# Three edits to hand-written instruction orders in the differential-attention part of a two-layer trunk: a score block issued earlier, a group-norm matmul issued later, a copy issued later

## The chip, the cores and the metric

The kernel runs on one core of a Trainium2 chip, in one launch. The metric is the device time of that core in microseconds (us), as the median of several executions; a profile of one execution stands beside it. The engines are PE (TensorE, matrix products), DVE (VectorE), ACT (ScalarE), POOL (GpSimd) and SP (SyncE, which issues most DMA transfers).

## The reference, cut to what matters

Two layers work on one sequence of 1024 tokens with 1024 features. Layer 0 mixes the tokens by differential attention, layer 1 by latent attention (MLA); each is followed by a gated MLP with a short convolution. All edits lie in layer 0's attention, which is this:

```python
def diff_attention(h, w_qkv, ..., subln_g, w_o, lambda_init, cos, sin):
    q, k, v = jnp.split(h @ w_qkv, 3, axis=-1)      # 8 heads, each two query/key maps of 64
    ...                                             # rotary on q and k, lam from four vectors
    def block(args):                                # 128 queries
        sc = jnp.einsum('bqhcd,bkhcd->bhcqk', qb, k).astype(jnp.float32) * scale
        p = masked_softmax(sc, chunk_mask(blk, s)[None, None, None])
        a = p[:, :, 0] - lam * p[:, :, 1]
        return jnp.einsum('bhqk,bkhe->bqhe', a.astype(v.dtype), v)
    ...
    o = rms_norm(o, subln_g) * (1.0 - lambda_init)  # the group norm, over a head's 128 features
    return o.reshape(b, s, D_MODEL) @ w_o
```

The input `h` is `rms_norm(x, attn_norm_g[0])`, so each token row is multiplied by a norm vector first.

## The kernel before

Every product of float32 values is made of three matmuls on high and low parts (`mm3`, lines 119 to 121: high by low, high by high, low by high).

**Steps.** The attention has 32 steps `t = 4h + p`: head `h`, query pair `p`. A pair is two rows of 128 queries, `j = 0` and `j = 1`; row `i = 2p + j` sees the first `n = 128(i + 1)` keys. For each step the code holds small pieces of work under letters: `S0`, `S1` the scores of the two rows (L1859: for both maps, on 64 partitions each, three passes of a pair of matmuls); `M` masks and takes the maximum (DVE, L1868 and L1869); `E` the exponentials (ACT, L1884); `I` the inverse of the sums (DVE, L1889, L1890); `C` scales the first map (POOL, L149, for pairs 0 and 1); `X` subtracts the second map (DVE, L1897); `T` transposes the result (PE, L1905), `H` and `L` split it into high and low (ACT L127, DVE L130); `A` multiplies by the values (PE); `O` copies out (ACT, L1933). At the end of every second pair comes the group norm: `Q1`, `Q2`, `Q3` square and split (ACT L1939, L1942, POOL L130), `F` sums over the 128 features with a matrix of ones (PE, L1950 and L1951), and `R`, `N` take the root and scale (ACT L1957 to L1961, DVE). A prime behind a letter means the step before, two primes the step before that; a plus means the step after.

**Projections.** Between these pieces stand the two halves of up to two projection units per step, `U` and `V`, which make a half of the next queries, keys or values: `U0` and `U1` are 24 matmuls into a PSUM bank with the tag `u`, of which there is one. For queries and keys, `Us` (a shuffle, DVE L596) and `Um` (times the cosine, DVE L600) read that bank, `Up` and `Ua` (POOL, L617) finish the rotary, `Uqh` and `Uql` (ACT L127, POOL L130) split the query. `V0` opens the same bank for the second unit.

**Order.** `da_steps` runs a row of letters per step under a hand-written schedule, so each of PE, DVE, ACT and POOL executes its instructions in exactly the order of the row. Rows 0 to 3 of `DA_SCORE` serve the pairs 0 to 3; `DA_SECOND` replaces row 1 at `t = 1`; the rows of `DA_END` serve the last steps, `t = 28` on, where the output projection's pieces (small letters, and `Y`, `Z`) are mixed in. The row of pair 1 serves `t = 5, 9, 13, 17, 21, 25`; at `t = 29` a row of `DA_END` is used.

**Score buffers.** Scores go to PSUM tiles of two banks with the tag `S`, of which there are two. For pairs 0 and 1 a row's two maps share one tile; for pairs 2 and 3 each map takes one, so that `S0` alone takes both.

**The start.** `FIRST` is the order before the steps. For tile `i` of 128 tokens: `Q` squares (ACT L157), `R` the root (DVE L164, POOL L167), `N` times the norm vector (DVE L439), `T`, `H`, `L` transposes and splits of a half (`a`, `b`; PE L447, ACT L127, DVE L130). `g` spreads the norm vector over a score tile in PSUM; `G` (ACT, L509) copies it from there to SBUF, where `N2` to `N7` read it. `p10a` and `p10b` are the two halves of the first key projection, which need the `a` halves and the `b` halves of tiles 0 and 1; `z` are filling matmuls on ones (L195).

Of the kernel before, what the change touches and what calls it, by code (L numbers as in the profile page):

```python
# [56 lines left out]
class Trunk:  # L57
# [234 lines left out]
    def steps(self, attend, units, prepare, n, apart=False):  # L292
# [33 lines left out]

    DA_SCORE = (
# [4 lines left out]
    )  # L332

    DA_SECOND = "S0 I1' Vc' H2'' M0 L2'' A1'' C0' X0' H3'' E0b L3'' U0 E0a A2'' Wh Vt' N3'''' A3'' O'' Wl' Q2'' C1' I0 X1' U1 C0 S1 X0 Us Vh' Q1'' T0' H0' Q3'' Up F'' Um M1 Ua Wl R1'' Vl' E1b V0 E1a L0' I1 A0' Uqh R2'' R3'' Uql C1 N1'' X1 V1 T1 T0 H0"

    DA_END = (
# [9 lines left out]
    def da_steps(self, attend, units, prepare, n, extra):  # L346
# [4 lines left out]
        with self.tc.manual_schedule(engines={E.PE, E.DVE, E.Activation, E.Pool}):  # L351
            for t in range(-1, first + len(self.DA_END)):
                while len(steps) < min(n, t + 2):
# [3 lines left out]
                    for name, u in zip("UV", units(x)):  # L357
                        steps[x].parts.update({name + part: f for part, f in u.items()})
                row = self.DA_SECOND if t == 1 else self.DA_SCORE[t % 4] if t < first else self.DA_END[t - first]
                for name in row.split():  # L360
# [6 lines left out]
        assert not extra and not any(s.parts for s in steps)  # L367

    FIRST = (
# [1939 lines left out]
```

## Time and the profile before

| | |
|---|---|
| median of 3 runs | 2386.59 us (2385.97 to 2387.23) |
| profiled execution, its own time | 2385.1 us |
| its span, first to last instruction | 2383.2 us |
| PE busy | 2349.0 us, 99% |
| DVE, ACT, POOL busy | 1917.6, 1245.7, 586.2 us |
| mean granted TensorE clock | 0.998 |
| start (`FIRST`) | to about 42 us |
| steps of layer 0's attention | about 42 to 472 us |

An instruction's start and end are given in us from the span's start. Matmuls overlap: the time one costs PE is the step from its start to the next one's start, not the duration in its row. "Idle before" names what the engine waited for.

### The profile page before, as it was taken

Reading aid. Unit: us, or ns where it says so; the run is one execution under the profiler, and the core shown is the slowest. Engines: PE = TensorE matmul, PEld = TensorE weight load, DVE = VectorE, ACT = ScalarE, POOL = GpSimd, SP = SyncE. Lnnn points to the kernel's source line nnn. Section 1 sums busy time; section 2 is a strip of 40 time slices with the busy share of each in tenths; the row PEclk is TensorE's granted clock in tenths of the full one; section 3 lists DMA queues with packets and bytes.
Section 4 is the critical chain, followed back from the end, with each engine's and each line's share of the span. In section 5 each row is a group of like instructions: output and inputs, shape, how many; then the busy total and the mean of one; then the engine's idle time right before and its main releaser. Section 6 shows DMA issues by size and latency. Waiting matters only on the chain.

```text
span 2383.2 us, 32951 instructions
## 1 busy us (share of the span) xinstructions
PE 2349.0 (99%) x12146; PEld 1979.3 (83%) x12146; DVE 1917.6 (80%) x3169; ACT 1245.7 (52%) x2301; POOL 586.2 (25%) x466
## 2 busy tenths in 40 slices
PE   9999999999999999999999999999999999999998
PEld 8888888788888888888898889988788888887886
DVE  6777877758888888899865888886588888888997
ACT  5666666735444444354444778775354444443544
POOL 4545444324000000000133666673320000000001
PEclk9999999999999999999999999999999999999999
DMA  3111111332222222652221211133322222227502
GB/s 147 40 36 36 49 36 54 115 111 102 94 83 80 80 89 80 234 167 92 83 99 56 71 32 39 41 98 106 114 74 95 80 80 80 89 80 282 177 1 80
DMA packets 95666, 213.42 MB, mean 90 GB/s; under 512 B 8712, under 2 KB 33936, under 8 KB 95504
## 3 DMA queue, kind: packets, MB, share of 16 engines
q1 hardware_dynamic: 86304, 183.51, 23.5%
q10 hardware_dynamic: 9200, 27.80, 3.2%
q8 instruction: 96, 1.57, 0.3%
q14 instruction: 66, 0.54, 0.1%
HBM read 158.85 MB, written 52.43 MB: 89 GB/s over the span
## 4 chain that ended last, share of the span: by engine, by line
PE 89%; DVE 5%; DMA 2%; issue 1%; POOL 1%; ACT 1%; SPq 0%; DVEq 0%; POOLq 0%; ACTq 0%
PE S L119 13%; PE S L121 13%; PE S L120 13%; PE b L119 8%; PE b L120 8%; PE b L121 8%; PE u L119 5%; PE u L121 4%; PE u L120 4%; PE S L1859 3%; PE b L263 2%; PE u L2015 1%; PE u L2014 1%; PE b L1905 1%; DVE s L130 1%
## 5 line engine op out<-in xcount | busy, mean ns | idle before, releaser
L167 POOL TENSOR_TENSOR st<-st,mhalf 128x1 f32<-128x1 f32 x56 | 35.3, 632 | 1299.1 <-DVE st L164 1290.6
L119 PE MATMUL S<-s,u 128*128 128x512 f32 (+1 forms) x800 | 302.1, 378 | 1.8 <-DVE s L130 1.8
L121 PE MATMUL S<-s,u 128*128 128x512 f32 (+1 forms) x800 | 301.2, 377 | 1.5 <-DVE u L130 0.8
L120 PE MATMUL S<-s,u 128*128 128x512 f32 (+1 forms) x800 | 301.0, 376 | 0.0
L127 ACT CAST u<-h 128x512 fp32r<-128x512 f32 (+1 forms) x194 | 115.9, 619 | 273.8 <-DVE h L1012 271.9
L119 PE MATMUL b<-s,u 128*128 128x512 f32 x588 | 230.8, 393 | 1.2 <-DVE s L130 0.4
L121 PE MATMUL b<-s,u 128*128 128x512 f32 x588 | 229.1, 390 | 0.0
L120 PE MATMUL b<-s,u 128*128 128x512 f32 x588 | 229.0, 389 | 0.0
L1069 DVE SCALAR_TENSOR_TENSOR u<-u,conv,u 128x1023 f32<-128x1023 f32 (+1 forms) x176 | 224.9, 1278 | 0.8 <-ACT u L1065 0.7
L149 POOL TENSOR_TENSOR u<-u,st 128x512 f32<-128x512 f32 (+7 forms) x160 | 172.2, 1085 | 158.2 <-DVE st L2000 106.7
L127 ACT CAST s<-u 128x512 fp32r<-128x512 f32 (+3 forms) x229 | 144.3, 663 | 94.0 <-PE u L121 26.4
L127 ACT CAST u<-b 128x512 fp32r<-128x512 f32 (+1 forms) x256 | 134.7, 547 | 93.3 <-PE b L1905 58.5
L130 DVE TENSOR_TENSOR u<-b,u 128x512 fp32r<-128x512 f32 (+1 forms) x256 | 158.5, 631 | 25.1 <-ACT u L127 24.0
L119 PEld LDWEIGHTS S<-s,u 128*128 128x128 f32 x800 | 150.5, 188 | 30.1 <-DVE s L130 2.4
L121 PEld LDWEIGHTS S<-s,u 128*128 128x128 f32 x800 | 150.5, 188 | 29.2 <-DVE u L130 1.0
L120 PEld LDWEIGHTS S<-s,u 128*128 128x128 f32 x800 | 150.5, 188 | 27.4
L119 PE MATMUL u<-s,s 128*128 128x512 f32 (+1 forms) x408 | 165.1, 405 | 0.9 <-DVE s L130 0.7
L121 PE MATMUL u<-s,s 128*128 128x512 f32 (+1 forms) x408 | 158.3, 388 | 0.0
L120 PE MATMUL u<-s,s 128*128 128x512 f32 (+1 forms) x408 | 157.6, 386 | 0.0
L130 DVE TENSOR_TENSOR s<-u,s 128x512 fp32r<-128x512 f32 (+2 forms) x204 | 138.9, 713 | 11.1 <-ACT s L127 10.7
L1072 ACT ACTIVATE u<-u 128x1024 f32<-128x1024 f32 x44 | 46.7, 1062 | 187.3 <-DVE u L1069 187.3
L130 DVE TENSOR_TENSOR u<-h,u 128x512 fp32r<-128x512 f32 x171 | 117.4, 687 | 32.6 <-ACT u L127 31.5
(288 smaller groups left out, 6382.5 us busy)
## 6 DMA issues: line engine op xcount, KB each, us to landing
u<-in_ffn_up SPq DMA_DIRECT2D x88, 512.0 KB, 4.1
g_d<-u ACTq DMA_DIRECT2D x44, 512.0 KB, 2.6
u<-in_ffn_down SPq DMA_DIRECT2D x66, 256.0 KB, 4.9
u<-g_d SPq DMA_DIRECT2D x62, 256.0 KB, 4.1
s<-in_da_wqkv SPq DMA_DIRECT2D x23, 512.0 KB, 3.3
x_d<-u SPq DMA_DIRECT2D x16, 512.0 KB, 2.9
s<-x_d SPq DMA_DIRECT2D x8, 1024.0 KB, 10.6
u<-o_d SPq DMA_DIRECT2D x24, 256.0 KB, 3.1
```

The source lines that it names most:

```text
L119: mm(out, lh, rl, start=first, stop=False, skip_group_check=onto)
L120: mm(out, lh, rh, start=False, stop=False, skip_group_check=onto)
L121: mm(out, ll, rh, start=False, stop=last, skip_group_check=onto)
L127: self.nc.scalar.copy(out, src)
L130: (eng or self.nc.vector).tensor_sub(out, src, hi.bitcast(F32))
L149: self.nc.gpsimd.tensor_mul(x, x, s.to_broadcast(list(x.shape)))
L167: nc.gpsimd.tensor_tensor(r, s, self.mhalf, ALU.pow)
L263: self.nc.tensor.transpose(ps[:, j * P : (j + 1) * P], probs[t][:, k : k + P], self.ident)
L1069: nc.vector.scalar_tensor_tensor(t[half][:, back:], u[half][:, : S - back], w, t[half][:, back:], ALU.mult, ALU.add)
L1072: nc.scalar.activation(t[0], t[0], AF.Silu)
L1859: nc.tensor.matmul(sc[c][:, b : b + m], q[rows, qp, qs], kt[rows, kp, :m], start=x == 0, stop=x == 2)
L1905: k.nc.tensor.transpose(ps[:, j * P : (j + 1) * P], self.e[t][0][:, c : c + P], k.ident)
```

## The change

- In row 1 of `DA_SCORE` and in `DA_SECOND`, `S1` moves from behind `U1 C0` to directly behind `S0`.
- In `DA_END`, `F` of step 27 moves from the end of the row of `t = 29` (as `F''`, behind `T0' H0'`) into the row of `t = 30`, directly behind `S0` (as `F'''`).
- In `FIRST`, `G` moves from between `T1b` and `L0b` to behind `H1a H1b`.

No instruction is added, removed or resized.

```diff
     DA_SCORE = (
...
-        "S0 I1' Vc' H2'' M0 L2'' A1'' C0' X0' H3'' E0b L3'' U0 E0a A2'' Wh Vt' N3'''' A3'' O'' Wl' Q2'' C1' I0 X1' U1 C0 S1 X0 Us Vh' Wl Q1'' T0' H0' Q3'' Up F'' Um M1 Ua R1'' Vl' E1b V0 E1a L0' I1 A0' Uqh R2'' R3'' Uql C1 N1'' X1 V1 T1 T0 H0",
+        "S0 S1 I1' Vc' H2'' M0 L2'' A1'' C0' X0' H3'' E0b L3'' U0 E0a A2'' Wh Vt' N3'''' A3'' O'' Wl' Q2'' C1' I0 X1' U1 C0 X0 Us Vh' Wl Q1'' T0' H0' Q3'' Up F'' Um M1 Ua R1'' Vl' E1b V0 E1a L0' I1 A0' Uqh R2'' R3'' Uql C1 N1'' X1 V1 T1 T0 H0",
...
-    DA_SECOND = "S0 I1' Vc' ... I0 X1' U1 C0 S1 X0 Us Vh' Q1'' T0' H0' Q3'' Up F'' Um M1 Ua Wl R1'' Vl' E1b V0 ... Uql C1 N1'' X1 V1 T1 T0 H0"
+    DA_SECOND = "S0 S1 I1' Vc' ... I0 X1' U1 C0 X0 Us Vh' Q1'' T0' H0' Q3'' Up F'' Um M1 Ua Wl R1'' Vl' E1b V0 ... Uql C1 N1'' X1 V1 T1 T0 H0"
...
     DA_END = (
...
-        "S0 M0 A1'' Up b3 E0a L3'' Ua A2'' X0' A3'' Uqh Uql I1 O'' X1' Q1'' Q2'' Q3'' T0' H0' F'' E0b L0' g0 c3",
-        "S0 h0 M0a I0' l0 C1' C0' R1''' E0a R2''' M0b g1 A0'' Y0 E0b X1' X0' S1 ...",
+        "S0 M0 A1'' Up b3 E0a L3'' Ua A2'' X0' A3'' Uqh Uql I1 O'' X1' Q1'' Q2'' Q3'' T0' H0' E0b L0' g0 c3",
+        "S0 F''' h0 M0a I0' l0 C1' C0' R1''' E0a R2''' M0b g1 A0'' Y0 E0b X1' X0' S1 ...",
...
     FIRST = (
-        "... H0a H0b T1a L0a T1b G L0b H1a H1b L1a z3 Q2 R2 L1b X5 p10a p10b "
+        "... H0a H0b T1a L0a T1b L0b H1a H1b G L1a z3 Q2 R2 L1b X5 p10a p10b "
```

More of the change, by code (lines that the diff above doesn't have):

```diff
@@ L332 @@
     )
-    DA_SECOND = "S0 I1' Vc' H2'' M0 L2'' A1'' C0' X0' H3'' E0b L3'' U0 E0a A2'' Wh Vt' N3'''' A3'' O'' Wl' Q2'' C1' I0 X1' U1 C0 S1 X0 Us Vh' Q1'' T0' H0' Q3'' Up F'' Um M1 Ua Wl R1'' Vl' E1b V0 E1a L0' I1 A0' Uqh R2'' R3'' Uql C1 N1'' X1 V1 T1 T0 H0"
+    DA_SECOND = "S0 S1 I1' Vc' H2'' M0 L2'' A1'' C0' X0' H3'' E0b L3'' U0 E0a A2'' Wh Vt' N3'''' A3'' O'' Wl' Q2'' C1' I0 X1' U1 C0 X0 Us Vh' Q1'' T0' H0' Q3'' Up F'' Um M1 Ua Wl R1'' Vl' E1b V0 E1a L0' I1 A0' Uqh R2'' R3'' Uql C1 N1'' X1 V1 T1 T0 H0"
     DA_END = (
         "O'' d0 Up X1' S1 S0 V0 R2''' Ua R3''' M1 d1 b0 b1 M0 c0 T0' V1 E1b N1''' T2' H0' L0' E1a c1 Ukh +S1 d2 Vc E0a N2''' b2 Ukl E0b N3''' T1' +U0 T3' H2' H1' +M1 I1 +U1 I0 c2 +E1b +E1a L2' L1' d3 +Us A0' +Um C1 C0 H3'",
[2 rows of a table removed]
[2 rows of a table added]
         "S0 I1' A0'' h2 C1' I0' A1'' Y1 C0' O'' M0a X1' X0' y1 g3 T0' Q1'' M0b E0a T2' H0' N3'''' T1' H1' E0b L0' I0 l2 C0 Z1 Q2'' L1' z1 H2' h3",
```

4 rows, old and new, of tables (DA_END, FIRST) are left out of this document.

## The prediction

> **What bounds the kernel now.** I read the page's engine shares first, then the chain that ended last, then PE's waits, then the timeline of each engine at the three places that the edits touch.
>
> ```profile
> PE 2349.0 (99%) x12146; PEld 1979.3 (83%) x12146; DVE 1917.6 (80%) x3169; ACT 1245.7 (52%) x2301; POOL 586.2 (25%) x466
> PE 89%; DVE 5%; DMA 2%; issue 1%; POOL 1%; ACT 1%; SPq 0%; DVEq 0%; POOLq 0%; ACTq 0%
> PE b L1950 <- POOL h L130: 2.2, 1, 2.2
> PE b L1905 <- DVE u L1897: 1.2, 2, 1.0
> ```
>
> The first two lines are the page's shares and its chain: PE is the bound from end to end, so an edit gains only what it takes out of PE's own time or waits, and loses whatever new wait it gives PE. The last two are rows of the waits (total, times, longest). F waits 2.2 us once for `Q3`'s subtraction on POOL: this is the `F''` that the second edit moves. Transposes wait 1.2 us in all for `X`, 1.0 of it once. In the steps PE otherwise hardly waits.
>
> **First edit: S1 behind S0, at seven steps** (t = 1, 5, 9, 13, 17, 21, 25). The work is the same six matmuls and their weight loads in the same score tile; no DMA is involved. The rows are PE's timeline at t = 5 (start, duration).
>
> ```profile
> 167.14 0.39 PE L120 MATMUL u<-s,s 128*128 128x512 f32 x1
> 167.37 0.39 PE L121 MATMUL u<-s,s 128*128 128x512 f32 x1
> 167.69 0.97 PE L1859 MATMUL S<-u,u 64*128 64x512 f32 x6
> 168.58 0.55 PE L1905 MATMUL b<-ident,u 128*128 128x128 f32 x3
> ...
> 169.44 0.40 PE L119 MATMUL u<-s,s 128*128 128x512 f32 x1
> ```
>
> `U1`'s last matmul starts at 167.37, `T0'` at 168.58. A 512-column matmul costs PE a step of 0.23 (167.14 to 167.37), so `S1` takes 168.58 - 167.37 - 0.23 = 0.98. It is three passes of two matmuls side by side, an estimated 3 x 0.23 = 0.69 if they follow one another bare. The rest, about 0.3, is the change into the 64-row shape and out again. Next to `S0`, already in that shape, one change in and out goes: a gain of 0.29 per step, 7 x 0.29 = 2.0 in all, if nothing else happens. The Trainium skill's page "TensorEngine Tiling (Array Packing)", under "Key Properties", says that a change of tiling mode drains the TensorE; the 0.3 agrees, and by that rule alone the edit is a gain. That is the first rival.
>
> What speaks against it is what `S1` covers now. It stands between `U1` and `V0`; in its new place it stands ahead of `A1''`, `U0`, `A2''`, `Vt'`, `A3''` and `U1`, and makes each of them late by its bare 0.70 (bounds: 0.69, and 0.98 as it costs alone). PE's timeline shows no idle time before the rows from `A1''` to `U1` at this step, so nothing there takes the delay up. DVE's timeline shows what hangs on `U1`:
>
> ```profile
> 167.80 0.74 DVE L596 STREAM_SHUFFLE h<-u 128x512 f32<-128x512 f32 x1
> 168.43 0.68 DVE L600 TENSOR_TENSOR h<-u,s 128x512 f32<-128x512 f32 x1
> 169.12 0.17 DVE L1868 MEMSET S<- 64x128 f32 x1
> 169.32 1.23 DVE L1869 TENSOR_REDUCE st<-S 128x2 f32<-128x1024 f32 x1
> ```
>
> `Us` starts 0.04 after `U1`'s last matmul ends (167.37 + 0.39), `Um` ends at 169.11, then `M1` follows in DVE's order although its scores end at 168.66: the early `S1` doesn't bring `M1` forward, since `Um` stands ahead of it. `V0` writes the one bank `u` that `Us` and `Um` read, so it can't start before 169.11; it starts at 169.44, 0.33 behind. At t = 1, where no `F` stands in between, that margin is gone already:
>
> ```profile
> 56.06 0.39 PE L121 MATMUL u<-s,s 128*128 128x512 f32 x1
> 56.38 0.96 PE L1859 MATMUL S<-u,u 64*128 64x512 f32 x6
> 57.27 0.55 PE L1905 MATMUL b<-ident,u 128*128 128x128 f32 x3
> 57.86 0.50 PE L119 MATMUL u<-s,s 128*128 128x512 f32 x1
> ...
> 57.12 0.68 DVE L600 TENSOR_TENSOR h<-u,s 128x512 f32<-128x512 f32 x1
> ```
>
> `Um` ends at 57.80 and `V0` starts at 57.86: it waits for the bank. With `U1` later by 0.70, `V0` is later by 0.70 there. At the six other steps `Um` ends at 169.81 and `V0` starts at about 169.87, later by 0.43. `F''` is no help: it stands behind `A3''`, `O''`, `Q1''`, `Q3''`, which are later by 0.70 too.
>
> Then comes a second wait. From `M1` the work goes on to `E1b`, `E1a` and `Uqh` on ACT, `Uql` and `C1` on POOL, `X1` on DVE, each behind the one before:
>
> ```profile
> 171.92 0.61 ACT L127 CAST u<-h 128x512 fp32r<-128x512 f32 x1
> ...
> 172.62 1.29 POOL L130 TENSOR_TENSOR u<-h,u 128x512 fp32r<-128x512 f32 x1 [1.34 <-ACT u L127]
> 173.86 1.05 POOL L149 TENSOR_TENSOR u<-u,st 128x512 f32<-128x512 f32 x1
> ...
> 174.94 0.75 DVE L1897 SCALAR_TENSOR_TENSOR u<-u,st 128x512 f32<-128x512 f32 x1 [0.42 <-POOL u L149]
> ...
> 175.65 0.98 PE L1905 MATMUL b<-ident,u 128*128 128x128 f32 x7
> ```
>
> `X1` ends at 175.69. The first transpose of `T1` (175.65) reads `X0`'s row; the second, a seventh of the way on at about 175.76, reads `X1`'s. So PE has no margin here even now, and since the whole chain from `U1` on is later by 0.70, PE is later by 0.70 at this point, whatever it was at `V0`. Behind it PE runs without waits, so nothing is caught up. Sum of the first edit: 7 x 0.70 = +4.9. Bounds: -2.0 (no wait at all), 7 x 0.98 = +6.9.
>
> **Second edit: F behind the next S0.** Two matmuls and a bank of tag `b` move past `S0` on PE; ACT's and POOL's order is as before.
>
> ```profile
> 447.33 0.50 PE L1950 MATMUL b<-h,ones 128*128 128x512 f32 x1 [2.23 <-POOL h L130]
> 448.00 1.31 PE L1859 MATMUL S<-u,u 64*128 64x512 f32 x12
> ...
> 449.62 0.41 PE L120 MATMUL b<-u,u 128*128 128x256 f32 x1
> ...
> 446.68 0.20 ACT L1884 ACTIVATION_READ_ACCUMULATOR u<-S,st 128x1 f32 x1
> ...
> 445.64:449.05 3.41, 1.72 (x14) 1.21 (x14) 2.03 (x2) 2.43 (x6) 2.97 (x3) 1.00 0.00 0
> 449.05:452.46 3.41, 3.41 (x15) 2.91 (x14) 2.97 (x8) 2.01 (x5) 2.28 (x3) 0.50 0.53 154
> ```
>
> What is late next: `S0` of pair 2 takes both score tiles, and the second is free only when `E0b` is read out, 446.68 + 0.20 = 446.88 (ACT's row). `S0`'s first matmul can go earlier, its second at about 446.93. From there it takes as long as now, 448.00 to 449.24, so `F` starts at 448.17, its input long there. `F` costs about 0.57 with its entry, and the second matmul of `A0''` starts at 448.86 instead of 449.62: 0.76 gained, not 2.2.
>
> The two last rows are stretches of the trace (PE busy, PEld, DVE, ACT, POOL, granted clock): PE is idle for half of the first, and in the next 3.41 us the granted clock is 0.50. At half clock these 3.41 us do the work of 1.7; some of it is entry into shapes, so I take 1.4 lost (bounds 0 and 1.7). With the change, one idle of about 1.9 stands there, broken by one score matmul, against 2.5 now; I take it that the clock stays up. Sum: -0.76 - 1.4 = -2.15. Bounds: -2.2 - 1.7 = -3.9, and 0. The Trainium skill, in "TensorE: Matmul & The Clock Gate", Part 1, has the clock halved after an idle window of about 3.4 us; here half a window was enough. By that rule the clock would have no part in it and the second edit would bring 0.76 alone; the row decides otherwise.
>
> **Third edit: G behind H1b.** One ACT copy of 1.02 moves past two casts; no DMA.
>
> ```profile
> 11.10 1.02 ACT L509 COPY s<-S 128x1024 f32<-128x1024 f32 x1
> 12.00 1.09 ACT L127 CAST s<-b 128x512 fp32r<-128x512 f32 x2
> 12.96 1.09 ACT L157 ACTIVATE u<-u 128x1024 f32<-128x1024 f32 x1
> ...
> 12.64 0.69 DVE L130 TENSOR_TENSOR s<-b,s 128x512 fp32r<-128x512 f32 x1 [0.71 <-ACT s L127]
> 14.17 0.15 DVE L164 TENSOR_SCALAR st<-st 128x1 f32<-128x1 f32 x1 [0.84 <-ACT u L157]
> 14.24 0.68 DVE L130 TENSOR_TENSOR s<-b,s 128x512 fp32r<-128x512 f32 x1
> ...
> 11.65 0.63 PE L447 MATMUL b<-ident,u 128*128 128x128 f32 x2
> 13.48 0.36 PE L119 MATMUL u<-s,s 128*128 128x256 f32 x1 [0.73 <-DVE s L130]
> 14.98 0.38 PE L119 MATMUL u<-s,s 128*128 128x256 f32 x1
> ```
>
> `H1a` and `H1b` go first, but `H1b` must wait for `T1b`, whose last transpose ends at 11.65 + 0.63 = 12.28. So ACT idles, `H1b` runs to about 12.9, `G` to 13.8, and `Q2` starts at 13.7 instead of 12.96. `L1a` and with it `p10a` come 0.5 earlier (12.95). But `R2` (L164) stands ahead of `L1b` in DVE's order and waits for `Q2`: `L1b` waits behind it even now, its input being ready at 13.09. `R2` goes to 14.92, `L1b` ends at 15.68, `p10b` starts at 15.74, not 14.98. `p10a`'s half microsecond is idled away and 0.76 lost on top. `N2`, which needs `R2`, is later as well, so it stays. Bounds: -0.73 (all of the idle before 13.48 gone), +1.02 (all of `G`).
>
> **Sum.** +4.9 - 2.15 + 0.76 = +3.5. The profiled execution took 2385.1, so 2388.6 for one like it; the median of the runs is 1.5 above it, and the clock's fall need not be in each of them. Against the median: 2386.59 + 3.5 = 2390.1, 0.15% more. I count 0.2%, 4.8 us, as what a measurement of this kernel tells from no change, so this is no change, on the slow side.
>
> **Rivals.** *Faster: the shapes' change decides* and `V0` and `T1` don't wait. Then -2.0 from the first edit, -3.9 at most from the second, nothing from the third: 2380.7. For it: the 0.3 per step is plain in the rows. Against it: `V0` at 57.86 sits on `Um`, `T1` on `X1`. It decides if `U1`'s delay is under 0.1 us. Chance 0.08.
>
> *Slower: the clock falls all the same.* One mechanism at t = 30: PE still idles about 1.7 of 3.41 us there, as much as in the stretch before 449.05, and if the clock drops again, the second edit keeps only 0.6 or so: 4.9 - 0.6 + 0.76 = +5.1, 2391.7. For it: the idle share is near that of the row. Against it: the idle is shorter in all and broken. It decides once the granted clock shows 0.50 behind t = 30. Chance 0.24.
>
> *Half the loss:* `T1`'s wait is absorbed, since the second transpose hangs on something other than `X1`; then 0.43 at six steps, 0.70 at one: +3.3, sum +1.9, 2388.5. Against it: 175.69 and 175.76 stand too near each other. Chance 0.08.
>
> **How the numbers follow.** My forecast has 0.60; by itself it would range over 2388.0 to 2391.3, from the runs' spread and `F`'s terms. With the slower rival and the half loss the range is 2386.5 to 2393.0. Faster by over 0.2%: the first rival, 0.08. Slower: 0.24. Between: 0.68.
>
> **What would show it.** In the profile after: a wait of the product behind `T0'` for L600 at seven steps, 0.2 to 0.7 each; more of L1905 waiting for L1897, at six steps; one head's distance to the next up by 0.7 us; no wait of L1950, but one of L1859 for ACT's L1884 near t = 30; granted clock 1.00 behind it; `p10b` about 0.76 later. I am wrong if heads get shorter, or if L600 ends before PE asks for the bank.

## The result, and the profile after

The changed kernel takes 2392.03 us in the median, against 2386.53 for the kernel before on the same chip: the medians are 5.5 us apart. Over all eleven runs of each, the ratio is 1.0026, with a 95% interval of 1.0019 to 1.0034; that is 6.2 us more (4.5 to 8.1). The forecast was 2390.1 with a range of 2386.5 to 2393.0, so the time lies inside the range, at the place of the slower rival (2391.7).

The page's shares, and two stretches of the trace (their length, then the busy time of PE, PEld, DVE, ACT and POOL, then the granted clock):

```profile
PE 2355.2 (98%) x12146; PEld 1982.5 (83%) x12146; DVE 1918.1 (80%) x3169; ACT 1245.6 (52%) x2301; POOL 586.2 (24%) x466
...
1024.00:1031.00 7.00, 6.50 (x22) 5.18 (x22) 7.00 (x12) 3.89 (x8) 0.00 (x0) 0.76 0.97 361
1700.00:1710.00 10.00, 7.33 (x24) 6.18 (x25) 6.03 (x6) 2.41 (x5) 1.81 (x2) 0.66 0.26 80
```

The work is the same to the instruction. This execution took 2398.55 us, 6.5 above the median, and its mean granted clock, 0.996, is the lowest of its eleven runs: the two stretches, far behind the edits, show a lowered clock that the profile of before doesn't have there (1.00 at 1021 to 1028 and at 1696 to 1706). So its span is not used below; the places of the edits are.

**First edit.** The rows between 167 and 176 us that the prediction calls `t = 5` are those of `t = 9`: the six `V0` of the row of pair 1 start at 114.30 (`t = 5`), 169.44 (`t = 9`) and so on to 389.97 (`t = 25`). The same row of letters serves all six, so its sums stand. Here are PE and then DVE of the changed kernel at `t = 9`, and PE at `t = 1`:

```profile
169.69 0.39 PE L121 MATMUL u<-s,s 128*128 128x512 f32 x1
169.93 0.49 PE L1905 MATMUL b<-ident,u 128*128 128x128 f32 x3
170.76 0.50 PE L1950 MATMUL b<-h,ones 128*128 128x512 f32 x1 [0.34 <-POOL h L130]
171.09 0.40 PE L1951 MATMUL b<-h,ones 128*128 128x512 f32 x1
171.48 0.50 PE L119 MATMUL u<-s,s 128*128 128x512 f32 x1
...
170.13 0.73 DVE L596 STREAM_SHUFFLE h<-u 128x512 f32<-128x512 f32 x1
170.76 0.67 DVE L600 TENSOR_TENSOR h<-u,s 128x512 f32<-128x512 f32 x1
...
58.82 0.50 PE L119 MATMUL u<-s,s 128*128 128x512 f32 x1 [1.07 <-DVE h L600]
```

`T0'` now follows `U1` at once. `S0` and `S1` together take 1.42 (160.33 to 161.75), where `S0` alone took 0.72 (158.70 to 159.42): `S1` costs the bare 0.70 of the prediction, and `U1` is late by that. `F''` waits for `Q3`; `V0` starts at 171.48, 0.05 behind `Um`'s end (170.76 + 0.67). At t = 1, without an `F`, the whole wait of 1.07 shows at `V0`. At t = 9 the waits list names only F's 0.34: `V0` itself waits too, but its wait is shorter than the tail of the matmul ahead of it, so it is no idle time. One reads it from the step, 171.09 to 171.48, where 0.24 did before (169.20 to 169.44). The step behind the wait is longer too: 0.34 (171.48 to 171.82) instead of 0.23. Then `X1` on DVE, and `T1` and `S0` on PE:

```profile
177.27 0.75 DVE L1897 SCALAR_TENSOR_TENSOR u<-u,st 128x512 f32<-128x512 f32 x1 [0.42 <-POOL u L149]
...
177.80 1.15 PE L1905 MATMUL b<-ident,u 128*128 128x128 f32 x7
178.88 0.50 PE L1859 MATMUL S<-u,u 64*128 64x512 f32 x2
```

`X1` ends at 178.02, inside the seven transposes, which now take 1.15 instead of 0.98: the second wait. As it falls inside a group of matmuls, the waits list doesn't show it either. The distance from head to head is read from `V0`, of which the first and the last of six stand here, for the kernel before and the changed one:

```profile
114.30 0.40 PE L119 MATMUL u<-s,s 128*128 128x512 f32 x1
389.97 0.40 PE L119 MATMUL u<-s,s 128*128 128x512 f32 x1
...
115.60 0.50 PE L119 MATMUL u<-s,s 128*128 128x512 f32 x1
394.95 0.50 PE L119 MATMUL u<-s,s 128*128 128x512 f32 x1
```

Before, (389.97 - 114.30) / 5 = 55.13 us; after, (394.95 - 115.60) / 5 = 55.87: 0.74 more per head. Of this, 0.69 arises in the step itself (from `S0` of t = 9 to `S0` of t = 10, 17.86 before and 18.55 after); the rest is spread over the head's other steps and isn't traced. At t = 1 it is 0.65 (16.73 and 17.38, from `S0` there to `S0` of t = 2).

**Second edit.** PE, ACT's end of `E0b`, and two stretches of 3.41 us:

```profile
449.99 0.44 PE L1905 MATMUL b<-ident,u 128*128 128x128 f32 x2 [0.20 <-DVE u L1897]
451.12 0.50 PE L1859 MATMUL S<-u,u 64*128 64x512 f32 x1 [0.69 <-POOL u L130]
452.23 1.90 PE L1859 MATMUL S<-u,u 64*128 64x512 f32 x11 [0.61 <-ACT u L1884]
454.06 0.79 PE L1950 MATMUL b<-h,ones 128*128 128x512 f32 x1
...
459.01 0.50 PE L1859 MATMUL S<-u,u 64*128 64x512 f32 x2
...
451.98 0.20 ACT L1884 ACTIVATION_READ_ACCUMULATOR u<-S,st 128x1 f32 x1
...
449.16:452.57 3.41, 1.90 (x12) 1.12 (x12) 1.66 (x6) 3.38 (x8) 2.52 (x2) 1.00 0.20 83
452.57:455.98 3.41, 3.41 (x18) 3.01 (x15) 2.96 (x7) 0.72 (x3) 3.23 (x4) 0.50 0.24 72
```

F waits no more; `S0`'s first matmul waits for `Uql`, its second for `E0b`. From the last transpose of `T0'` (450.15, the second of the group) to `S1` of t = 30 (459.01) it takes 8.86 us, against 9.54 before (444.84 to 454.37): 0.68 gained, with the clock at 0.50 for 3.41 us in both. The two edits account for the steps: from the first score matmul of t = 0 to the last of t = 31 it takes 432.29 us against 427.95 before, 4.3 more, and 6 x 0.74 + 0.65 - 0.68 is 4.4.

**Third edit.** ACT, DVE and PE at the start:

```profile
9.78 1.55 ACT L127 CAST s<-b 128x512 fp32r<-128x512 f32 x3
11.83 0.59 ACT L127 CAST s<-b 128x512 fp32r<-128x512 f32 x1 [0.50 <-PE b L447]
13.22 1.07 ACT L157 ACTIVATE u<-u 128x1024 f32<-128x1024 f32 x1
...
14.41 0.15 DVE L164 TENSOR_SCALAR st<-st 128x1 f32<-128x1 f32 x1 [2.13 <-ACT u L157]
...
15.22 0.39 PE L119 MATMUL u<-s,s 128*128 128x256 f32 x1 [1.14 <-DVE s L130]
```

ACT idles 0.50 ahead of `H1b`, `Q2` is late, `R2` waits 2.13 on DVE with `L1b` behind it, and `p10b` waits 1.14.

### The profile page after: what moved, and what is told of

Its sections match the earlier page's. It is cut to its first block, busy times and chain, and to the rows that moved or that the text cites. A ratio compares the mean times of both kernels' runs of the same rounds, so it can differ in the third digit from the quotient of the medians.

```text
span 2396.8 us, 32943 instructions
## 1 busy us (share of the span) xinstructions
PE 2355.2 (98%) x12146; PEld 1982.5 (83%) x12146; DVE 1918.1 (80%) x3169; ACT 1245.6 (52%) x2301; POOL 586.2 (24%) x466
## 4 chain that ended last, share of the span: by engine, by line
PE 88%; DVE 5%; DMA 3%; ACT 2%; issue 1%; POOL 1%; SPq 0%; POOLq 0%; DVEq 0%; ACTq 0%
PE S L119 13%; PE S L121 13%; PE S L120 13%; PE b L119 8%; PE b L120 8%; PE b L121 8%; PE u L119 5%; PE u L121 4%; PE u L120 4%; PE S L1859 3%; PE b L263 2%; PE u L2015 1%; PE u L2014 1%; PE b L1905 1%; DVE s L130 1%
## 5 line engine op out<-in xcount | busy, mean ns | idle before, releaser
L130 DVE TENSOR_TENSOR u<-b,u 128x512 fp32r<-128x512 f32 (+1 forms) x256 | 158.7, 632 | 25.4 <-ACT u L127 24.1
L130 DVE TENSOR_TENSOR s<-u,s 128x512 fp32r<-128x512 f32 (+2 forms) x204 | 139.2, 717 | 12.3 <-ACT s L127 12.0
L130 DVE TENSOR_TENSOR u<-h,u 128x512 fp32r<-128x512 f32 x171 | 117.5, 687 | 32.6 <-ACT u L127 31.5
```

The source lines that it names most:

```text
L130: (eng or self.nc.vector).tensor_sub(out, src, hi.bitcast(F32))
```

## The experiments

**Each edit alone.** Of each edit, the place to which the piece moves:

```diff
e1_s1:  S0 S1 I1' ... U1 C0 X0 Us      (both rows of pair 1)
e2_f:   ... T0' H0' E0b L0' g0 c3   and   S0 F''' h0 M0a ...
e3_g:   ... L0b H1a H1b G L1a ...
```

> The first edit alone: S1 directly behind S0 in the row of pair 1 and in the row of t = 1. Theory (the chain that begins with U1 is late by S1's bare length): the distance from head to head goes from 55.14 to 55.86 us, V0 starts 1.79 behind U1's last matmul and waits for Um, the second transpose of T1 waits for X1, and the time is about 5.0 us above the kernel before, 0.2%. Rival (the loss comes from the other two edits, and one change of shape less is a gain): heads shorter by about 0.3, time 2 us below before.

> The second edit alone: F behind the next S0. Theory: S0's second matmul waits for E0b, as in the changed kernel; the stretch from the last transpose of T0' to the second matmul of A0'' gets shorter by 0.5 to 0.8 us if the clock is full over it, and the granted clock may fall to 0.50 behind it or not: 0.6 to 2.2 us below before. Rival (the wait for F is simply gone): that stretch is 2.2 shorter, and no wait of L1859 for ACT's L1884.

> The third edit alone: G behind H1b. Theory (R2 stands ahead of L1b on DVE and waits for Q2 behind G): p10b starts about 0.76 us later after the first x tile's norm N0 than in the kernel before, with a wait of over 1 us ahead of it, and the kernel is about 0.8 us slower, which the times can hardly tell. Rival (an earlier L1a is a gain): p10b starts at the old distance from N0 or up to 0.7 earlier.

Measured: `S1` alone 1.0023 (1.0014 to 1.0033), 5.5 us more; `F` alone 0.9995 (0.9986 to 1.0003); `G` alone 1.0006 (0.9997 to 1.0015). The first edit is the loss; the others can't be told from nothing in the times, and the three ratios together give 1.0024. The rows: `V0` of the first and last of six heads with `S1` alone, then PE with `F` alone, then the start of `p10b` with `G` alone and with `S1` alone:

```profile
114.32 0.50 PE L119 MATMUL u<-s,s 128*128 128x512 f32 x1
393.82 0.50 PE L119 MATMUL u<-s,s 128*128 128x512 f32 x1
...
444.97 0.50 PE L1859 MATMUL S<-u,u 64*128 64x512 f32 x1 [0.69 <-POOL u L130]
446.10 1.24 PE L1859 MATMUL S<-u,u 64*128 64x512 f32 x11 [0.63 <-ACT u L1884]
...
447.97 0.28 PE L120 MATMUL b<-u,u 128*128 128x256 f32 x1
...
451.38 0.50 PE L1859 MATMUL S<-u,u 64*128 64x512 f32 x2
...
15.01 0.39 PE L119 MATMUL u<-s,s 128*128 128x256 f32 x1 [1.14 <-DVE s L130]
...
14.01 0.38 PE L119 MATMUL u<-s,s 128*128 128x256 f32 x1
```

With `S1` alone the heads are 55.90 apart, and the steps from t = 0 to t = 31 take 5.2 us more than before (433.12). With `F` alone the waits are those of the changed kernel, and here the clock stayed up: 7.4 us from `T0'` (its last transpose at 444.00) to `S1` at 451.38, where the changed kernel took 8.86. So this edit gains 0.7 if the clock falls in both kernels and 2.2 if it falls in the first alone. The prediction's own distance, to the second matmul of `A0''`, is 3.97 (444.00 to 447.97) against 4.78 before (444.84 to 449.62): 0.81 less.

With `G` alone, `p10b` starts 5.44 behind `H0a` (15.01 and 9.57) against 4.85 with `S1` alone, which has `G` in its old place (14.01 and 9.16): 0.59 lost. The changed kernel has 5.44 as well, and ten of the eleven profiles with `G` in its old place have 4.84 to 4.88. The eleventh is the kernel before itself, with 5.22 (14.98 and 9.76); against it the loss is 0.22. In that execution the transposes of the start still took 0.42 us each instead of 0.27, because its clock came up to 1.00 only at 12.14 us, in the others between 6.0 and 9.5; so `H0b` and `T1b` were late.

**Two waits in a row.** `M1` goes ahead of `Us` on DVE, so that `X1` no longer hangs behind `Um`.

```diff
-... U1 C0 X0 Us ... Up F'' Um M1 Ua ...
+... U1 C0 X0 M1 Us ... Up F'' Um Ua ...
```

> The first edit, and M1 moved on DVE from behind Um to ahead of Us, where DVE idles and M1's scores are there already. V0 still waits for Um, but X1 no longer hangs on M1 behind Um. Theory of two waits in a row (V0 on Um, then T1 on X1): V0's wait stays, T1's goes, and a head is 0.5 longer than before instead of 0.72: 3.5 us above before. Rival (X1's chain alone sets the head): the head is back at 55.14 or below. Other rival (Um alone sets it): 0.72 stays.

Measured: 1.0018 (1.0009 to 1.0027). `V0`, first and last, and `T1` at t = 9:

```profile
114.79 0.50 PE L119 MATMUL u<-s,s 128*128 128x512 f32 x1
392.88 0.50 PE L119 MATMUL u<-s,s 128*128 128x512 f32 x1
...
176.74 0.92 PE L1905 MATMUL b<-ident,u 128*128 128x128 f32 x7
```

The heads are (392.88 - 114.79) / 5 = 55.62 apart, 0.49 above before, and the seven transposes take 0.92 without a gap. Both waits are real: `V0`'s alone costs 0.49, `X1`'s makes it 0.74 to 0.77. Both rivals fell: the head is neither back at 55.14 nor left at 0.72 above it.

**A smaller delay.** `Vt'` also goes behind `U1`, which makes `U1` late by 0.26 instead of 0.70.

```diff
-... A2'' Wh Vt' N3'''' A3'' ... X1' U1 C0 X0 M1 Us Vh' Wl Q1'' ...
+... A2'' Wh N3'''' A3'' ... X1' U1 Vt' C0 X0 M1 Us Wl Q1'' Vh' ...
```

> As the kernel with M1 ahead of Us, and Vt' (four transposes, 0.44 us of PE) moved from ahead of U1 to behind it, with Vh' behind Q1'' on ACT so that the group norm is not held up. U1 is then late by 0.70 - 0.44 = 0.26 instead of 0.70, and V0's margin before the change was 0.27. Theory (the loss is U1's delay, passed on through Um's hold on the bank u): the heads are back at 55.14 to 55.3, the wait of F goes, and the time is 0 to 1 us above before; the 0.3 of the change of shape is not yet earned, since V0 still stands on Um. Rival (the loss is in holding both score tiles from the row's start, or in anything else that goes with S1's place): the heads stay at 55.6.

```profile
114.06 0.50 PE L119 MATMUL u<-s,s 128*128 128x512 f32 x1 [0.36 <-DVE h L600]
391.01 0.50 PE L119 MATMUL u<-s,s 128*128 128x512 f32 x1 [0.35 <-DVE h L600]
...
1695.23 1.09 PE L811 MATMUL b<-ident,u 128*128 128x128 f32 x8 [2.95 <-DVE u L914]
```

55.39 us: 0.26 above before. The loss shrinks with `U1`'s delay, from 0.49 to 0.26, with `S1` in the new place all the while, so the place of `S1` and its hold on the score tiles are not the cause of what went. The forecast of no loss to 0.2 missed by a little: `M1`, now ahead of `Us`, ended 0.2 too late for it (`Us` starts at 168.05, `U1`'s last matmul ends at 167.82).

The time, 1.0020 (1.0011 to 1.0029), 4.8 us, is higher than the 0 to 1 us expected, and higher than the heads say. In the profile the excess isn't in the attention, whose steps take 428.22 us, 0.3 more than before. It comes in one place 1200 us behind the edits, in the last row: there PE waits 2.95 for DVE's L914, which waited 3.32 for a DMA transfer (0.25 and 1.72 in the profile of before), and the clock fell behind it. Whether the other executions lost their time there too, and whether the edits have a part in it, is open.

**E0b's hold, and the clock.** `E0b` ahead of `H0'`; then, in the kernel before, nine filling matmuls in F's bank; then both ideas together.

```diff
e6_f_e0b:      ... Q3'' E0b T0' H0' L0' g0 c3   with F behind S0
e7_fill:       in total(), for h == 6 and p == 3, ahead of F's two matmuls:
+    for _ in range(9):
+        k.nc.tensor.matmul(self.ss, k.ones, self.heads[7]["k"][0][:, 0, :], start=True, stop=True)
e10_end_fill:  e6_f_e0b, and five such matmuls into sc[0] ahead of the first of S0's at t = 30
```

> The second edit, and E0b on ACT moved from behind H0' to ahead of it, so that S0's second score tile comes free 0.36 us earlier. Theory (E0b's hold on the tile is what took the place of F's wait): from the last transpose of T0' to the first matmul of S1 at t = 30 it takes 7.0 us at full clock, against 7.4 with the second edit alone, and the wait of L1859 for ACT's L1884 is under 0.3 us; the time is about 2.5 below before. Rival (S0 waits for something else, such as Uql): the wait stays at 0.6.

> The kernel before with nine more matmuls of ones by a ready key tile into F's own bank, put ahead of F, in the 2.2 us in which PE waits for F's input; F itself overwrites the bank, so no result changes. It tells the price of the idle time from that of the clock behind it. Theory (the clock falls because PE idles for half of a stretch of 3.41 us): F starts when it did, 2.5 behind the last transpose of T0', the granted clock stays 1.00 up to t = 31, and from that transpose to S1 at t = 30 it takes 8.1 us instead of 9.5; 1.4 below before. Rival (the clock falls there for another reason): 0.50 again, and 9.5 us.

> The second edit with E0b ahead of H0', and five matmuls of ones by a ready key tile put ahead of the first of S0's at t = 30, into the score tile that S0 then overwrites. With E0b ahead alone the clock fell at that place in its profile although PE idled only about 1.3 us. Theory (idle share of the stretch sets the clock): 1.00 behind t = 30, and 7.0 to 7.2 us from the last transpose of T0' to S1 at t = 30; 2.4 below before. Rival (the clock falls there whatever fills it): 0.50 and 8.5 us.

Measured: 0.9996 (0.9987 to 1.0004), 0.9990 (0.9981 to 0.9998) and 0.9990 (0.9981 to 0.9999). The rows: `S0`'s second matmul and two stretches with `E0b` ahead; the filling matmuls, F and `S1` in the kernel before; F and three stretches of the kernel with the smaller delay above, where F's wait of 2.23 is still there:

```profile
446.19 1.12 PE L1859 MATMUL S<-u,u 64*128 64x512 f32 x4 [0.27 <-ACT u L1884]
442.92:446.33 3.41, 2.13 (x13) 1.37 (x14) 1.29 (x5) 3.29 (x9) 2.40 (x3) 1.00 0.43 157
446.33:449.74 3.41, 3.41 (x16) 2.91 (x17) 3.09 (x8) 0.92 (x3) 3.24 (x3) 0.50 0.05 14
...
444.26 2.35 PE L1952 MATMUL b<-u,ones 128*128 128x512 f32 x9
446.77 0.50 PE L1953 MATMUL b<-h,ones 128*128 128x512 f32 x1 [0.17 <-POOL h L130]
452.22 0.51 PE L1859 MATMUL S<-u,u 64*128 64x512 f32 x2
...
448.45 0.50 PE L1950 MATMUL b<-h,ones 128*128 128x512 f32 x1 [2.23 <-POOL h L130]
443.76:447.17 3.41, 2.13 (x15) 1.49 (x13) 1.93 (x6) 2.92 (x7) 2.41 (x3) 1.00 0.64 233
447.17:450.59 3.42, 2.14 (x16) 1.57 (x17) 2.14 (x3) 2.02 (x5) 3.24 (x3) 1.00 0.03 12
450.59:454.00 3.41, 3.41 (x20) 2.62 (x19) 3.23 (x7) 2.49 (x6) 1.87 (x3) 1.00 0.57 156
```

`E0b` ahead cuts `S0`'s wait from 0.63 to 0.27, as expected. But the clock fell behind it all the same, so its profile doesn't show the 7.0 us, and the runs don't show the 2.5 us less: 1.0 less is not clear of none. Filled, F starts 2.5 behind `T0'` as before, the clock stays at 1.00, and `S1` follows 8.0 after the last transpose (444.24) instead of 9.54: the fall alone costs 1.5, and filling the wait is a gain though F starts no sooner. With both, the clock stayed up too, but the stretch took 7.45 us (444.05 to 451.50), not the 7.0 to 7.2 expected. The kernel takes 2383.31 us against 2386.04. It is the version to keep, without the first and third edits: faster than the kernel before by 0.1%, with an interval that only just leaves out 1. That it is better than the filled kernel before isn't shown.

The last rows show why the fall can't be counted on: with F's wait at the full 2.23, the clock stayed at 1.00. Within one execution the changes of the clock lie whole numbers of 3.413 us apart: in the kernel before at 449.05, 452.46 and 2377.58, the last 565 such stretches behind the first. Counted back from a change at 1696.41, the stretches of this execution cut F's wait in two, and neither half idled as long as the stretch ahead of the fall in the kernel before.

By place, only the profiled executions show the clock. But every timed run has its mean granted clock, in thousandths, and one fall, half the clock for 3.41 of 2386 us, takes 0.0007 from it. With `F` alone the runs have 0.9975 on average against 0.9973 for the kernel before on the same chip, and with `E0b` ahead 0.9977 against 0.9976: moving F took away a fraction of a fall per run at most. With the filling matmuls it is 0.9987 against 0.9976, and with both ideas 0.9985 against 0.9973: more than one fall per run went. Why more than one is open.

**A row after the theory, and new waits.** `A3''` and `Vt'` behind `U1`, `F''` behind `V0`, `C1` ahead of `Uql` and `Wl`, `M1` ahead of `Us` (e8, with the end of e6), behind `Um` (e9), and e9 with the end of e10 (e11).

```diff
e8:  ... X1' U1 A3'' O'' Q2'' Vt' C0 X0 M1 Us Wl Q1'' Vh' T0' H0' E1b E1a Q3'' Up Um Ua Vl' V0 F'' L0' I1 C1 ... Uql X1 N1'' V1 T1 T0 H0
e9:  ... X1' U1 A3'' O'' Q2'' Vt' C0 X0 Us Wl Q1'' Vh' T0' H0' Q3'' Up Um M1 E1b E1a Ua Vl' V0 F'' L0' I1 C1 ... Uql X1 N1'' V1 T1 T0 H0
```

> A version after the theory: S1 behind S0; A3'' and Vt' moved behind U1, so that U1 is 0.44 earlier than before the change and V0 is covered; F'' behind V0; M1 ahead of Us; C1 ahead of Uql and, at t = 1, ahead of Wl on POOL, so that X1 comes earlier; at the end F behind S0 with E0b ahead of H0'; G as before. Theory: heads at 54.8 to 54.9 (the change of shape earned), the 1.0 of T1's wait at t = 1 gone, and 5 us below before in all. Rival (another wait comes up, for a bank of tag b or for Q3 on POOL): heads at 55.1 or above, and 2 to 3 us below before from the end alone.

> The rows of the version after the theory once more, with M1 back behind Um, because in that version Us started 0.9 us behind U1's end, held up by M1 on DVE; the end of the attention as in the kernel before. Theory (the loss is what delays Us and Um, whatever it is): Us 0.04 behind U1 again, V0 covered but for 0.1, heads at 54.85 to 55.0 against 55.14 before and 56.18 with M1 ahead of Us, T1's wait of 1.0 at t = 1 still gone; 2 to 3 us below before. Rival (the bank of tag b that N1'' frees late, or Q3, sets the head): heads at 55.5 or above.

> Both together: the rows with A3'' and Vt' behind U1 and M1 behind Um, and the end with E0b ahead and five filling matmuls. If both theories hold the gains add: 4.5 to 5.5 us below before, 0.2%; if the heads have a wait of their own again, about 2 below from the end alone, less what the heads lose.

Measured: 1.0024 (1.0015 to 1.0033), 1.0035 (1.0022 to 1.0047, six runs) and 1.0014 (1.0006 to 1.0023). None gained: the heads are 56.16 (e8) and 56.20 (e9) apart, above what the rivals named, and the third is 3.3 us above before, where its two forecasts were gains. In e8 the wait is one that neither theory nor rival named: `Us` stands behind `M1`; `U1`'s last matmul ends at 166.17, `Us` starts at 167.11 (first row), and `V0` waits 0.87 to 1.03 for `Um`. In e9 `Up` stands behind `Q3`, which `A3''` now makes late, on POOL (second row), as its rival said; then `Uql` and `X1` run side by side on POOL and DVE, and `T1` waits 0.59 for `X1`:

```profile
167.11 0.72 DVE L596 STREAM_SHUFFLE h<-u 128x512 f32<-128x512 f32 x1
...
169.83 1.30 POOL L130 TENSOR_TENSOR h<-h,h 128x512 fp32r<-128x512 f32 x1 [3.16 <-ACT h L1939]
...
174.70 1.29 POOL L130 TENSOR_TENSOR u<-h,u 128x512 fp32r<-128x512 f32 x1
...
174.78 1.77 DVE L1897 SCALAR_TENSOR_TENSOR u<-u,st 128x512 f32<-128x512 f32 x1 [2.37 <-POOL u L149]
...
176.60 0.44 PE L1905 MATMUL b<-ident,u 128*128 128x128 f32 x2 [0.59 <-DVE u L1897]
```

`X1` takes 1.77 here and 1.76 in e8 (at 173.43), with `Uql` beside it both times; it takes 0.75 in the kernel before, where POOL is free at that time (174.94). At 0.75 it would end at 175.53 in e9, ahead of the second transpose's turn, and `T1` wouldn't wait. So putting `C1` ahead of `Uql` brought its own cost. That POOL's work is what stretches `X1` fits these rows, but no edit tested it by itself. Whether the 0.3 of the shapes' change can be earned at all stays open.

**R2 and L1b.** `L1b` goes ahead of `R2`, with `G` in its new place.

```diff
-... H1a H1b G L1a z3 Q2 R2 L1b X5 ...
+... H1a H1b G L1a L1b z3 Q2 R2 X5 ...
```

> The third edit, and L1b moved on DVE ahead of R2. Theory (p10b waited only because L1b stands behind R2, which waits for Q2 behind G; N2 is late by the same): p10b's wait goes, it starts 1.5 behind p10a, but the transposes of tile 2 wait for N2 instead, and are 6.7 to 6.9 us behind the start of H0a, against 6.97 with G behind H1b and 6.37 to 6.41 with G in its old place. Rival (p10b's wait was the whole loss): 6.4 again.

Measured: 1.0002 (0.9993 to 1.0011). `p10b` starts 1.51 behind `p10a` (13.37 and 11.86), without a wait; the transposes of tile 2 wait 1.03 and start 6.79 behind `H0a` (16.00 and 9.21), against 6.97 with `G` alone (16.54 and 9.57) and 6.37 with `S1` alone (15.53 and 9.16); the kernel before, with its late `H0b`, has 6.76. `N2`'s lateness behind `G` was the second wait, as expected.

## Why the prediction was right, and where a term was off

The sign and the mechanism were right, the size was short: +3.5 us was forecast, 5.5 to 6.2 measured. The main forecast by itself ranged to 2391.3, and 2392.03 lies above that; the stated range holds it because it was widened for the slower rival. Of the three outcomes that the prediction set out, the measured one, 0.23 to 0.26% more, is on the side of "slower by over 0.2%", which had 0.24.

The first edit: right in both waits, in their places and nearly in size. The bare 0.70 per step was measured as 0.69 within the step, and as 0.74 per head in the changed kernel and 0.77 with `S1` alone; +4.9 was forecast for the edit, 5.5 measured (3.3 to 7.9). "Half the loss" fell: the kernel with `M1` ahead shows what a head costs when `T1` doesn't wait. The faster rival fell at its own point, `U1`'s delay of 0.70. Two expected signs were misread beforehand. The waits list doesn't name L600 at the six steps, because `F''` waits first, for L130 on POOL, and `V0`'s wait hides in a matmul's tail. And L1905's waits for L1897 are 1.2 us, twice, as before, because `X1`'s hides among the seven transposes.

The second edit: 0.76 forecast; with `F` alone the same distance shrank by 0.81, and in the changed kernel the stretch to `S1` shrank by 0.68, by the very wait that was named, `E0b`. The step that failed is "I take it that the clock stays up", with its 1.4 us: in the changed kernel's profile it fell. With `F` alone it stayed up in the profile, but the mean clock of the timed runs shows hardly a fall less than before. The slower rival's sum (+5.1) fits better than the forecast's (+3.5). Where in the timed runs of the changed kernel the clock fell isn't known, so how much of the missing 2 to 2.7 us is the clock's stays open.

The third edit: 0.76 forecast, 0.59 measured against the other profiles with `G` in its old place, again by the wait named. That the sizes are so near is luck in part: the sum was made on the rows of an execution whose transposes were slow at the start, and it put `p10b` 5.98 behind `H0a` (15.74 and 9.76), where 5.44 was measured.

## What to carry to other kernels

In an order written by hand, a piece that PE does early pushes back everything between its new and its old place; before moving it, list who reads those pieces and what PE next needs of theirs, for here six matmuls that were a cover cost more than twice what their joining could earn. A consumer in strict order (`M1` behind `Um`) got nothing from an input that came sooner. And a piece moved on one engine can land beside one of another and slow it, as `Uql` beside `X1`. A wait that can't be removed may still be filled: filling matmuls moved nothing and gained 0.1% (0.02 to 0.19).

## What the runs showed of the hardware

The clock fell to 0.50 for 3.41 us behind stretches in which PE was busy for 1.72, 1.90 and 2.13 us of 3.41, but not behind two others of 2.13 and 2.14, so PE's busy time in the profile alone does not decide it. With `E0b` ahead, the stretch before the fall had waits of 0.69, 0.27 and 0.18 us and 0.15 of other idle time: no single long wait was needed. The fall cost 1.5 us (9.54 against 8.0 with the wait filled).

`X1` took 1.77 us on DVE with a POOL instruction beside it (e9), and 0.75 without (the kernel before).
